# A decoder step on one core: attention taken by pairs of heads over all four query blocks, in a written order on the array, with its memory laid out by hand

## The chip, the core and the metric

The kernel runs on one core of one Trainium2 chip. The core has five engines that run their own instruction streams and meet by semaphores: PE (the matmul array; its weight loads are shown as PEld), DVE (vector), ACT (scalar activation), POOL (general) and SP (which issues transfers). The metric is the device time of one execution in microseconds (us). The three timed executions of the kernel before took 2037.08, 2037.58 and 2037.85 us; the median is 2037.58.

## The reference

One inference step of a decoder layer, for 512 prompt tokens with 16 learned tokens ahead of them, and for 8 sample tokens with a cache of 128 positions each. With D = 2048:

```
z = LN(x) @ w_in + b_in                      # columns: q 16 x 64 | k 4 x 64 | v 4 x 64 | u 1024
q, k = rope(q), rope(k)                      # the first 16 of 64 dims are rotated
s = q k^T / 8, masked to 128 positions back and self; m = max(max s, sink); p = exp(s - m)
attn = p v / (sum p + exp(sink - m))         # 4 heads share one k and v
d_g = mean over the last 2, 4, 8, 16 positions of u_g, minus u_g       # 4 groups of 256 channels
pool_g = (d_g @ w_pool_g) * scale
h1 = LN(alpha h + [attn, pool] @ w_o)
y  = LN(alpha h1 + (silu(h1 @ w_gate) * (h1 @ w_up)) @ w_down)         # inner width 5632
```

Outputs are y for prompt and sample rows, the last keys and values, and the last 15 rows of u. All is float32.

## The kernel before, in words

**Products.** Channels lie on the 128 partitions, tokens on the free axis. The 536 token columns (8 sample, 16 learned, 512 prompt) go as two halves of 276 and 260, and behind attention, without the learned ones, as two of 260. A float32 product is made of three products of the faster type fp32r: each weight and each operand is split into a leading and a trailing part, and `products` issues leading × leading (L97), weight leading × operand trailing (L98) and weight trailing × operand leading (L100). Weights are split while the kernel runs: 512 columns at a time, ACT casts the leading part (`wh`, L91) and DVE subtracts to get the trailing one (`wl`, L92). Both come from rings of WB = 7 tiles.

**Attention's stage.** After the first layer norm, its transposes and the blocks of keys and values come eight blocks of queries (`mm_q`; a block is 128 columns of w_in, that is a pair of heads) and eight of pool input (`mm_u`); each is 96 matmuls. DVE adds the bias to a block of queries (L345) and rotates it (L280 to L283). `attention` (L354) takes one pair of heads, in two half groups of two query blocks each: scores (L369, float32, 64 rows of the array for each of the two heads), maxima with the mask on DVE (L372), exponentials on ACT (L381), scaling (L392), transposes (`tp`, L398 to L406), a copy by ACT, values (`o`, L412). Half groups share two banks of PSUM for scores, one for transposes and one for values; four banks belong to the blocks. `pool_group` (L469) takes the windowed differences (`dh`, `dl`) of two blocks of u through the group's map (`pm`). `sample_attention` does the eight sample rows with very small matmuls.

**Behind it.** `out_proj` (L593) makes `o` for the two halves of the rows; `ln1` (L620) is a layer norm over partitions by matmuls with ones (mean L624, var L633, whose squares `sq` come from ACT), then DVE and POOL make the operands T1 to T4 of a Winograd form (L641 to L660, parts split at L618). Gate and up take two 128-column blocks and both halves of rows at once by seven products of 24 matmuls (class `Set`; p1 to p7). The second layer norm, that of half 1, stands beside NFILL = 8 parts `fill()`: products 1 and 2 of the first eight sets, which need only half 0. Then come 44 sets, the down projection in four chunks, and the closing layer norm.

**Order.** The Tile framework orders each engine's instructions by dependencies, priorities and a timeline of its own. On an engine they run in that order. In the stage of attention it is this that places scores, transposes and values inside the blocks of products.

Of the kernel before, what the change touches and what calls it, by code (L numbers as in the profile page):

```python
# [7 lines left out]
F32 = mybir.dt.float32  # L8
# [29 lines left out]
NFILL = 8  # L38
LP = 600
STEP = 6  # L40
WB = 7
NRAW = 5
NT = 6
NG = 56

# [4 lines left out]
HALF = [slice(0, HN), slice(HN, NTOK)]  # L50
DHALF = [slice(0, NS + 256), slice(NS + 256, NTOK)]
# [3 lines left out]
def hybrid_step(ctx, tc, xin, w_in, w_o, w_g, w_u, w_d, w_pool, par_d, cst_d, ident_d, ln2gb, kct_d, vc_d, hist_d,  # L55
# [3 lines left out]
    cp = ctx.enter_context(tc.tile_pool(name="cp", bufs=1))  # L59
    wp = ctx.enter_context(tc.tile_pool(name="wp", bufs=2))  # L60
    ap_ = ctx.enter_context(tc.tile_pool(name="ap", bufs=16))
    dp = ctx.enter_context(tc.tile_pool(name="dp", bufs=1, space=bass.MemoryType.DRAM))

# [10 lines left out]
    def row_tile(name, w=NTOK):  # L74
        """[128, 520] float32 from the shared ring."""
        return ap_.tile([P, NTOK], F32, tag="row", name=name, bufs=16)[:, :w]

    # ---------------------------------------------------------------- weights
# [6 lines left out]
    def split(s, name, lo=None):  # L85
        """float32 [128, <=512] -> its leading and trailing float32r parts."""
        n = s.shape[-1]
        wh = wp.tile([P, 512], F32R, tag="wh", name=f"wh_{name}", bufs=WB)[:, :n]
        wl = wp.tile([P, 512], F32R, tag="wl", name=f"wl_{name}", bufs=WB)[:, :n]
        with tc.high_priority(prio[0]):  # L90
            nc.scalar.copy(wh, s)  # L91
            (lo or nc.vector).tensor_sub(wl, s, wh.bitcast(F32))  # L92
        return wh, wl
# [29 lines left out]
    def rstd_of(pool, var, n, name):  # L123
        """1/sqrt(var + eps) with one Newton step."""
        w = var.shape[-1]
        if w < HN:
            ve, r, t = [pool.tile([P, 3], F32, tag=f"rs{i}", name=f"rs{i}_{name}", bufs=3)[:n, :w] for i in range(3)]
        else:
            ve, r, t = [pool.tile([P, HN], F32, tag="t", name=f"rs{i}_{name}", bufs=NT) for i in range(3)]
# [17 lines left out]
    # ================================================================ phase A  # L147
    mixf = {}
    with ExitStack() as sa:
        act = sa.enter_context(tc.tile_pool(name="act", bufs=1))  # L150
        pa = sa.enter_context(tc.tile_pool(name="pa", bufs=1))
# [14 lines left out]
        xe = [wp.tile([P, 1024], F32, tag="raw", name=f"xe{c}", bufs=NRAW) for c in range(2)]  # L166
# [29 lines left out]
        def stats_e():  # L196
            """The same on the scalar engine for the 20 + 4 rows: the mean, then the mean square about it."""
# [33 lines left out]
        def x_half(h):  # L231
# [5 lines left out]
            for k2 in range(KT // 2):  # L237
# [13 lines left out]
                for kk in range(2):  # L251
                    k = 2 * k2 + kk
                    c, ks = k // 4, slice((k % 4) * P, (k % 4 + 1) * P)
                    tp = aux_tile([P, 512], ["sc", "sc", "pt", "o"][k % 4], f"xt{h}_{k}", 2 if k % 4 < 2 else 1)
# [30 lines left out]
        # ---- keys and values  # L285
# [3 lines left out]
        ko = pa.tile([P, 256], F32, tag="pts", name="ko", bufs=2)  # L289
        kvs = pa.tile([P, 2, 256], F32, tag="pts", name="kvs", bufs=2)[:NS]  # L290
# [15 lines left out]
        nc.sync.dma_start(cst, cst_d)  # L306
        prio[0] = WPRIO
# [29 lines left out]
        # the sample rows' queries: the two heads of a block in columns of their own, zero in the other's rows  # L337
# [16 lines left out]
        def attention(t, q):  # L354
            kt = t // 4
            mixf[t] = row_tile(f"mixf{t}")
            for bh in range(2):
                nm_ = f"{t}_{bh}"
                s = pa.tile([P, 2, 2, 256], F32, tag="s", name=f"s{nm_}", bufs=2)
                st = pa.tile([P, 4, 2, 2], F32, tag="sst", name=f"sst{nm_}", bufs=2)  # L360
                mx, nm, den, es = st[:, 0], st[:, 1], st[:, 2], st[:, 3]
                sc = [aux_tile([P, 2, 256], "sc", f"sc{nm_}_{j}", 2) for j in range(2)]
                for bb in range(2):
                    b = 2 * bh + bb
                    n, k0 = (NB0, 0) if b == 0 else (256, C_P + P * (b - 1))
                    mask = cst[:, CM0:CM0 + NB0] if b == 0 else cst[:, CM1:CM1 + 256]
                    for j in range(2):
                        r = slice(64 * j, 64 * j + 64)
                        nc.tensor.matmul(sc[j][:, bb, :n], q[r, C_P + P * b:C_P + P * (b + 1)], kT[r, kt, k0:k0 + n],  # L369
                                         start=True, stop=True)  # L370
                    for j in range(2):
                        nc.vector.tensor_tensor_reduce(out=s[:, bb, j, :n], in0=sc[j][:, bb, :n], in1=mask, scale=1.0,  # L372
                                                       scalar=NEG, op0=ALU.add, op1=ALU.max,
                                                       accum_out=mx[:, j, bb:bb + 1])
                sink = [par[:, PSINK + HEAD_A[t] + 4 * j:PSINK + HEAD_A[t] + 4 * j + 1] for j in range(2)]
# [11 lines left out]
                o = aux_tile([P, 2, P], "o", f"o{nm_}", 1)  # L387
                for bb in range(2):
                    b = 2 * bh + bb
                    n = NB0 if b == 0 else 256  # L390
# [3 lines left out]
                    tp = aux_tile([P, 2, 2, P], "pt", f"tp{t}_{b}", 1)  # L394
                    pt = pa.tile([P, 2, 2, P], F32, tag="pts", name=f"pts{t}_{b}", bufs=2)
                    if b == 0:
                        for j in range(2):
                            nc.tensor.transpose(tp[:META, 0, j, :], s[:, 0, j, 0:META], ident)  # L398
                            nc.tensor.transpose(tp[:, 1, j, :], s[:, 0, j, C_P:C_P + P], ident)
                        nc.scalar.copy(pt[:META, 0], tp[:META, 0])  # L400
                        nc.scalar.copy(pt[:, 1], tp[:, 1])
                        chunks = [(4, META), (0, P)]
                    else:
                        for j in range(2):
                            for c in range(2):
                                nc.tensor.transpose(tp[:, c, j, :], s[:, bb, j, c * P:(c + 1) * P], ident)  # L406
                        nc.scalar.copy(pt, tp)
                        chunks = [(b - 1, P), (b, P)]
                    for j in range(2):
                        kv = 2 * kt + j  # L410
                        for c, (vch, kn) in enumerate(chunks):
                            nc.tensor.matmul(o[64 * j:64 * j + 64, bb, :], vtm[:kn, vch, kv * 64:kv * 64 + 64],  # L412
                                             pt[:kn, c, j, :], start=(c == 0), stop=(c == 1))
                nc.vector.tensor_copy(mixf[t][:, NS + 256 * bh:NS + 256 * (bh + 1)], o.rearrange("p a b -> p (a b)"))

        # ---- pooling; its rows in the order sample, meta, prompt
# [555 lines left out]
```

## Time and profile before

| | |
|---|---|
| median of three executions | 2037.58 us (2037.08 to 2037.85) |
| profiled execution: span | 2037.3 us |
| PE busy | 1980.5 us, 97% |
| DVE busy | 1394.9 us, 68% |
| ACT busy | 890.6 us, 44% |
| POOL busy | 71.5 us, 4% |
| first PE instruction | 19.9 us |
| first query block to the last pooling map | 95 to 391 us |
| output projection | 391 to 587 us |
| second layer norm, until PE runs at full rate | 587 to 674 us |

The only execution profiled has the span above; the timed ones include what lies around it. A row of the timeline gives start and duration of one instruction, engine, line, operation, output and inputs, and in brackets the idle time before it with what ended it. Durations of matmuls overlap, so the distance of starts is what one costs. A float32 matmul leaves two records, one of fp32r one. "granted clock" (PEclk) is the share of full speed that the array was given.

### The profile page before, as it was taken

How to read it: one execution, taken by the hardware profiler on the slowest of the kernel's cores; microseconds unless marked ns; L12 is line 12 of the kernel's file. 1: busy time of each engine (PE TensorE's matmuls, PEld its weight loads, DVE VectorE, ACT ScalarE, POOL GpSimd, SP SyncE). 2: the span in 40 equal slices, each digit the busy share in tenths (PEclk: the TensorE clock that was granted, in tenths of full speed). 3: DMA queues.
4: the chain of work that ended last, by engine and by line, in shares of the span. 5: the costliest groups of instructions: out<-in, count | busy, mean ns of one | idle time of the engine just before them, and what ended most of it. 6: DMA issues, size and time to landing. Idle time of an engine off the chain costs nothing.

```text
span 2037.3 us, 39750 instructions
## 1 busy us (share of the span) xinstructions
PE 1980.5 (97%) x16059; PEld 1928.7 (95%) x16059; DVE 1394.9 (68%) x2815; ACT 890.6 (44%) x1854; POOL 71.5 (4%) x71
## 2 busy tenths in 40 slices
PE   5999999999998999999999999999999999999996
PEld 4988888999998999999999999999999999999996
DVE  6655556765869998888788888888875342332586
ACT  6533344543646545445444545444543232222342
POOL 3100000000007100000000000000000000000000
PEclk9999999999999999999999999999999999999998
DMA  7722112375744454343333334333456343432554
GB/s 279 223 66 64 60 61 68 130 223 174 237 149 156 141 182 156 108 132 112 117 118 122 120 110 128 112 127 107 133 185 210 105 138 101 153 96 94 161 165 143
DMA packets 104968, 278.38 MB, mean 137 GB/s; under 512 B 12792, under 2 KB 35904, under 8 KB 104744
## 3 DMA queue, kind: packets, MB, share of 16 engines
q1 hardware_dynamic: 104784, 275.85, 41.6%
q8 instruction: 125, 2.05, 0.4%
q14 instruction: 59, 0.48, 0.1%
HBM read 250.93 MB, written 27.41 MB: 137 GB/s over the span
## 4 chain that ended last, share of the span: by engine, by line
PE 94%; DVE 4%; ACT 1%; issue 1%; DMA 1%; SPq 0%; DVEq 0%; ACTq 0%
PE p_u L100 7%; PE p_u L97 7%; PE p_u L98 7%; PE p_g L100 7%; PE p_g L98 7%; PE p_g L97 7%; PE d L100 6%; PE d L98 6%; PE d L97 6%; PE o L100 3%; PE o L97 3%; PE o L98 3%; PE mm_q L97 2%; PE mm_q L98 2%; PE mm_u L97 2%; PE mm_q L100 2%
## 5 line engine op out<-in xcount | busy, mean ns | idle before, releaser
L98 PE MATMUL d<-al,wh_d 128*128 128x260 f32 x1056 | 274.6, 282 | 0.0
L97 PE MATMUL d<-ah,wh_d 128*128 128x260 f32 x1056 | 273.8, 282 | 0.0
L92 DVE TENSOR_TENSOR wl_u<-raw_u,wh_u 128x512 fp32r<-128x512 f32 x316 | 212.1, 693 | 54.5 <-ACT wh_u L91 51.3
L91 ACT CAST wh_u<-raw_u 128x512 fp32r<-128x512 f32 x316 | 185.4, 620 | 113.9 <-DVE raw_u L692 106.4
L91 ACT CAST wh_g<-raw_g 128x512 fp32r<-128x512 f32 x284 | 164.6, 621 | 134.5 <-DVE raw_g L692 123.7
L92 DVE TENSOR_TENSOR wl_g<-raw_g,wh_g 128x512 fp32r<-128x512 f32 x284 | 192.0, 696 | 33.7 <-ACT wh_g L91 30.5
L100 PE MATMUL d<-ah,wl_d 128*128 128x260 f32 x1056 | 212.5, 283 | 0.0
L98 PEld LDWEIGHTS d<-al,wh_d 128*128 128x128 f32 x1056 | 198.3, 188 | 0.0
L97 PEld LDWEIGHTS d<-ah,wh_d 128*128 128x128 f32 x1056 | 198.0, 188 | 0.0
L100 PEld LDWEIGHTS d<-ah,wl_d 128*128 128x128 f32 x1056 | 162.5, 188 | 0.0
L91 ACT CAST wh_d<-raw_d 128x512 fp32r<-128x512 f32 x144 | 82.3, 583 | 174.5 <-PE d L100 140.0
L97 PE MATMUL o<-mh,wh_o 128*128 128x260 f32 x512 | 145.1, 286 | 0.0
L98 PE MATMUL o<-ml,wh_o 128*128 128x260 f32 x512 | 144.9, 284 | 0.0
L100 PE MATMUL o<-mh,wl_o 128*128 128x260 f32 x512 | 144.9, 284 | 0.0
L834 DVE TENSOR_TENSOR acc<-acc,d 128x260 f32<-128x260 f32 x64 | 24.3, 422 | 153.9 <-PE d L100 153.9
L692 DVE TENSOR_TENSOR raw_g<-raw_g,raw_g 128x512 f32<-128x512 f32 x152 | 103.4, 693 | 0.6
L692 DVE TENSOR_TENSOR raw_u<-raw_u,raw_u 128x512 f32<-128x512 f32 x152 | 102.4, 685 | 1.8 <-DMA raw_u<-in_w_u_dram 1.2
L98 PEld LDWEIGHTS o<-ml,wh_o 128*128 128x128 f32 x512 | 97.1, 190 | 0.1
L100 PEld LDWEIGHTS o<-mh,wl_o 128*128 128x128 f32 x512 | 97.1, 190 | 0.0
L97 PEld LDWEIGHTS o<-mh,wh_o 128*128 128x128 f32 x512 | 96.6, 190 | 0.1
L91 ACT CAST wh_o<-raw_o 128x512 fp32r<-128x512 f32 x128 | 73.3, 616 | 48.0 <-DMA raw_o<-in_w_o_dram 34.7
L92 DVE TENSOR_TENSOR wl_d<-raw_d,wh_d 128x512 fp32r<-128x512 f32 x144 | 86.9, 641 | 4.9 <-ACT wh_d L91 3.8
(496 smaller groups left out, 6464.9 us busy)
## 6 DMA issues: line engine op xcount, KB each, us to landing
raw_g<-in_w_g_dram SPq DMA_DIRECT2D x96, 512.0 KB, 4.5
raw_u<-in_w_u_dram SPq DMA_DIRECT2D x96, 512.0 KB, 4.1
raw_o<-in_w_o_dram SPq DMA_DIRECT2D x64, 512.0 KB, 4.6
raw_d<-in_w_d_dram SPq DMA_DIRECT2D x48, 512.0 KB, 3.6
a_d<-c_g SPq DMA_DIRECT2D x44, 260.0 KB, 2.1
af<-a_d SPq DMA_DIRECT2D x44, 260.0 KB, 4.0
raw_d<-in_w_d_dram SPq DMA_DIRECT2D x48, 192.0 KB, 2.4
raw_kv<-in_w_in_dram SPq DMA_DIRECT2D x16, 512.0 KB, 4.7
```

What stands on the lines that cost most here:

```text
L91: nc.scalar.copy(wh, s)
L92: (lo or nc.vector).tensor_sub(wl, s, wh.bitcast(F32))
L97: nc.tensor.matmul(o, wh, hi[j], start=first, stop=False)
L98: nc.tensor.matmul(o, wh, lo[j], start=False, stop=False)
L100: nc.tensor.matmul(o, wl, hi[j], start=False, stop=last)
L692: op(t[:, gs], a[:, gs], b[:, gs])
L834: nc.vector.tensor_add(t, t, o)
```

## The change

**Attention over all four query blocks.** `attention` becomes four functions. `att_scores` issues the eight score matmuls of a pair (four blocks, two heads) into four banks, `att_softmax` does the two half groups, `att_turn` the sixteen transposes and `att_values` the sixteen value matmuls into one bank. The blocks of products now have two banks instead of four, the transposes share the four of the scores.

**A written order.** `step(engine)` makes every instruction issued inside it depend, on that engine, on the last twelve of the step before, without a semaphore. The stage's PE work is written as such steps: first block of queries, scores of pair 0, then in each round a block, transposes of the pair, a block, and values of that pair with scores of the next. Pooling maps stand behind the transposes of rounds 3 and 5 and in round 7, and the sample rows' pieces in between.

**Memory by hand.** Instead of pools there are three regions cut into rings by offsets. The rings of `wh` and `wl` have 4 tiles in attention's stage and 5 behind it (7 before); the ring of `hb`, `sq` and the helpers of 1/sqrt 3 (6 before); NFILL is 6 (8 before), with three pairs of sets instead of four made ahead; transposed probabilities have 4 tiles (2), the differences `dh` and `dl` 3 (2). The rows of the input beyond four tiles of 128 no longer lie in the weight ring. The down projection's inputs go through the ring of the fills. What the kernel computes is the same.

```diff
-NFILL = 8
+NFILL = 6
-WB = 7
+WA = 4
+WB = 5
-NT = 6
+NT = 3
...
+    @contextmanager
+    def step(*engines):
+        block = nc.cur_bb.bb
+        last = block.instructions[-1]
+        yield
+        code = block.instructions
+        start = next(k for k in reversed(range(len(code))) if code[k] is last) + 1
+        new = {}
+        for i in code[start:]:
+            if i.engine in [e.engine for e in engines]:
+                new.setdefault(i.engine, []).append(i)
+                for j in behind.get(i.engine, ()):
+                    tc.add_manual_dep(i, j, mybir.DependencyInfo(mybir.DependencyClass.NoSync,
+                                                                 mybir.DependencyReason.DATA), reason="step")
+        behind.update({e: [i.name for i in v][-12:] for e, v in new.items()})
...
         def mm_tile(name):
-            return ps.tile([P, 512], F32, tag="mm", name=name, bufs=4)
+            return ps.tile([P, 512], F32, tag="mm", name=name, bufs=2)
...
+        def att_scores(t, q):
+            kt = t // 4
+            sc = [[aux_tile([P, 2, 256], "sc", f"sc{t}_{bh}_{j}", 4) for j in range(2)] for bh in range(2)]
+            for b in range(4):
+                n, k0 = (NB0, 0) if b == 0 else (256, C_P + P * (b - 1))
+                for j in range(2):
+                    r = slice(64 * j, 64 * j + 64)
+                    nc.tensor.matmul(sc[b // 2][j][:, b % 2, :n], q[r, C_P + P * b:C_P + P * (b + 1)],
+                                     kT[r, kt, k0:k0 + n], start=True, stop=True)
+            return sc
...
+        def att_turn(t):
+            pts[t] = []
+            for b in range(4):
+                s, bb = soft[t][b // 2], b % 2
+                tp = aux_tile([P, 2, 2, P], "sc", f"tp{t}_{b}", 4)
+                pt = pa.tile([P, 2, 2, P], F32, tag="pts", name=f"pts{t}_{b}", bufs=4)
...
-        qq = [q_block(0), q_block(1)]
-        for t in range(8):
-            attention(t, qq[t])
-            if t < 6:
-                qq.append(q_block(t + 2))
-            if t > 0:
-                pool_step(t - 1)
-        sample_attention()
-        pool_step(7)
+        block("q0")
+        order = ["q1 q2", "q3 u0", "q4 u1", "q5 u2", "q6 u3", "q7 u4", "u5 u6", "u7"]
+        for t in range(8):
+            with step(pe):
+                if t:
+                    att_values(t - 1)
+                sc = att_scores(t, qs.pop(t))
+                if t >= 6:
+                    next(sample)
+            att_softmax(t, sc)
+            done, us = us, []
+            if t == 7:
+                with step(pe):
+                    for u in done:
+                        next(u)
+                    next(pool_group(2))
+            for n, name in enumerate(order[t].split()):
+                if n == 1:
+                    with step(pe):
+                        att_turn(t)
+                        for u in done:
+                            next(u)
+                        if t == 6:
+                            next(sample)
+                    if t in (3, 5):
+                        with step(pe):
+                            next(pool_group((t - 3) // 2))
+                block(name)
...
-        zs = pb.tile([P, HN], F32, tag="t", name=f"zs{h}", bufs=NT)
+        zs = pb.tile([P, HN], F32, tag="zs", bufs=2)
```

Line numbers in the changed kernel: products L185, L186 and L188; trailing split L180; bias L433; rotation L367 to L370; scores L452; transposes L496 to L503; mean L770, var L779. Its buffers carry the names of the regions (`fr`, `rr`, `mid_a`, `mid_b`).

Three places of the engines' orders show what moves. First PE before, inside the fifth block of queries: `sc2` are scores of pair 2, `mm_q4` the block.

```order
L100 MATMUL mm_q4_1_2031<-xhi1_121,wl_q4_01_2063 128x260
L369 MATMUL sc2_1_0_1982<-kT_124,q2_1544 128x256
L97 MATMUL mm_q4_0_2030<-xhi0_120,wh_q4_01_2062 128x276
...
L98 MATMUL mm_q4_0_2030<-xlo0_122,wh_q4_10_2092 128x276
L369 MATMUL sc2_1_1_1983<-kT_124,q2_1544 128x256
L97 MATMUL mm_q4_1_2031<-xhi1_121,wh_q4_10_2092 128x260
```

And PE of the change, around the scores of pair 0, between the first and the second block of queries:

```order
L188 MATMUL mm_q0_0_902<-rr_61 128x276
L188 MATMUL mm_q0_1_903<-rr_61 128x260
L452 MATMUL sc0_0_0_1018<-mid_a_62 128x152 [waits DVE_49,Activation_49]
L452 MATMUL sc0_0_1_1019<-mid_a_62 128x152
L452 MATMUL sc0_0_0_1018<-mid_a_62 128x256
L452 MATMUL sc0_0_1_1019<-mid_a_62 128x256
L452 MATMUL sc0_1_0_1020<-mid_a_62 128x256
L452 MATMUL sc0_1_1_1021<-mid_a_62 128x256
L185 MATMUL mm_q1_0_1066<-rr_61 128x276
L186 MATMUL mm_q1_0_1066<-rr_61 128x276
```

Scores that stood alone among products now follow one another, and those of pair 0 stand ahead of the second block. Second, DVE of the change at that place, from the bias of the first block to its rotated queries:

```order
L433 TENSOR_SCALAR mid_a_62<-mm_q0_0_902,fr_60 128x276 [waits PE_49]
L433 TENSOR_SCALAR mid_a_62<-mm_q0_1_903,fr_60 128x260 [waits PE_49]
L180 TENSOR_TENSOR rr_61<-fr_60,rr_61 128x512 [waits Activation_49]
L367 STREAM_SHUFFLE fr_60<-mid_a_62 128x536 [waits DMAHW0_49,DVE_49]
L368 TENSOR_TENSOR fr_60<-fr_60,mid_a_62 128x536 [waits DVE_49]
L369 TENSOR_TENSOR mid_a_62<-mid_a_62 128x536
L370 TENSOR_TENSOR mid_a_62<-mid_a_62,fr_60 128x536 [waits DVE_49]
```

One split of weights stands among them, where there were two. Third, PE in the second layer norm: before,

```order
L100 MATMUL p1_g0_7126<-b11h2_4475,wl_g0_11_7146 128x260
L633 MATMUL var1_7044<-sq1_1_7050,onesd_67 128x260 [waits Activation_49]
L633 MATMUL var1_7044<-sq1_2_7054,onesd_67 128x260 [waits Activation_49]
L633 MATMUL var1_7044<-sq1_3_7058,onesd_67 128x260 [waits Activation_49]
L633 MATMUL var1_7044<-sq1_4_7062,onesd_67 128x260 [waits Activation_49]
L633 MATMUL var1_7044<-sq1_5_7066,onesd_67 128x260 [waits Activation_49]
L97 MATMUL p1_g0_7126<-b11h3_4477,wh_g0_11_7145 128x260
```

and in the change:

```order
L185 MATMUL p2_g0_6110<-mid_b_3823,rr_61 128x260
L779 MATMUL var1_6017<-fr_60 128x260 [waits Activation_49]
L186 MATMUL p2_g0_6110<-mid_b_3823,rr_61 128x260
L779 MATMUL var1_6017<-fr_60 128x260 [waits Activation_49]
L188 MATMUL p2_g0_6110<-mid_b_3823,rr_61 128x260
L185 MATMUL p2_g0_6110<-mid_b_3823,rr_61 128x260
L779 MATMUL var1_6017<-fr_60 128x260 [waits Activation_49]
```

The sum of squares now comes in pieces of mostly one matmul among the products of the fills.

More of the change, by code (lines that the diff above doesn't have):

```diff
@@ L409, in attention @@
-                    for j in range(2):
[L410 to L414, printed above, removed]
+                soft[t].append(s)
@@ new lines, in hybrid_step @@
+        with step(pe):
+            att_turn(7)
+            next(sample)
+        g3 = pool_group(3, True)
+        for p in range(2):
+            with step(pe):
+                next(g3)
+                next(us[0])
+                if p == 0:
+                    att_values(7)
+                    next(sample)
+    for p in (sp[0], act, pa):
+        p.close()
+    sp[:] = [Pool(rr), WB]
+    for t in ("wh", "wl"):
+        sp[0].ring(t, 512, F32R, WB)
+    pb, gp = Pool(fr), Pool(rr, Region("mid_b", F32R, MDW))
```

224 lines of the change are left out of this document (142 added, 82 removed).

## The prediction

> **What bounds the kernel now.** I read the page from the top, then the windows, the waits of PE, and single rows of the timeline. First the page: the busy shares, the slices of PE and of its granted clock, and the chain that ended last.
>
> ```profile
> span 2037.3 us, 39750 instructions
> PE 1980.5 (97%) x16059; PEld 1928.7 (95%) x16059; DVE 1394.9 (68%) x2815; ACT 890.6 (44%) x1854; POOL 71.5 (4%) x71
> PE   5999999999998999999999999999999999999996
> PEclk9999999999999999999999999999999999999998
> PE 94%; DVE 4%; ACT 1%; issue 1%; DMA 1%; SPq 0%; DVEq 0%; ACTq 0%
> ```
>
> PE is the bound, and 97% leaves only 57 us of idle. But "busy" hides two things: what PE does between its products, and at which clock. So next the windows, cut at the stages (95 first query block, 391 output projection, 587 second layer norm, 674 full rate again). Columns: PE, weight load, DVE, ACT and POOL busy with counts, then the granted clock.
>
> ```profile
> core 0: us, PE busy (x) PEld busy (x) DVE busy (x) ACT busy (x) POOL busy (x), PEclk, DMA share, GB/s
> 95.00:391.00 296.00, 294.01 (x2272) 257.51 (x2271) 166.53 (x530) 110.02 (x323) 0.00 (x0) 0.99 0.23 73
> ...
> 602.00:648.00 46.00, 43.19 (x344) 42.51 (x343) 45.06 (x71) 30.23 (x68) 26.30 (x26) 0.96 0.48 153
> 648.00:674.00 26.00, 18.29 (x98) 16.49 (x98) 26.00 (x29) 13.01 (x32) 22.90 (x23) 0.74 0.16 49
> 700.00:725.00 25.00, 25.00 (x211) 25.00 (x210) 24.20 (x48) 11.35 (x21) 0.00 (x0) 1.00 0.59 187
> ```
>
> The last row is the steady state: 211 products in 25 us, 0.1185 us each. Two stages are off it. In 95 to 391 PE is busy throughout with 257 us of weight loads in 294; that is the stage of attention. In 602 to 674 it lost time openly: 2.8 + 7.7 us idle, and 344 and 98 products that need 40.8 and 11.6 us at the steady rate were busy for 43.2 and 18.3, so 9.1 us went to a low clock. PE's waits from 391 to 700 name what ended them (total, times, longest):
>
> ```profile
> PE p_g L100 <- DVE wl_g L92: 4.0, 3, 3.4
> PE p_g L98 <- DVE t3l L618: 3.7, 3, 2.3
> PE var L633 <- ACT sq L632: 3.2, 2, 1.9
> PE p_u L100 <- DVE wl_u L92: 2.6, 1, 2.6
> PE mean L624 <- DVE zs L608: 1.0, 1, 1.0
> ```
>
> Waits for var and mean make up 4.2 us, of which 1.9 belong to the first layer norm (the longest); so 2.3 us more were lost just behind 587, and the second layer norm costs 21.9 us now.
>
> **The attention stage: what is removed.** PE's timeline, one head pair's score inside a query block, then scores of both heads together:
>
> ```profile
> 123.28 0.29 PE L97 MATMUL mm_q<-xhi,wh_q 128*128 128x276 f32 x1
> 123.50 0.70 PE L369 MATMUL sc<-kT,q 64*128 64x256 f32 x2
> 124.12 0.39 PE L98 MATMUL mm_q<-xlo,wh_q 128*128 128x276 f32 x1
> 124.35 0.28 PE L97 MATMUL mm_q<-xhi,wh_q 128*128 128x260 f32 x1
> ...
> 151.91 0.70 PE L369 MATMUL sc<-kT,q 64*128 64x256 f32 x4
> 152.54 0.39 PE L98 MATMUL mm_q<-xlo,wh_q 128*128 128x260 f32 x1
> ```
>
> Each float32 matmul leaves two records. Between 123.28 and 124.35 lie 1.07 us; the two products take 0.25, so the lone score cost 0.82. A pair on the two halves of the rows (x4) takes 0.63 from its start to the next product, no more than one alone. So 0.63 is the work, and about 0.19 the way out of the products and back. From the orders of both kernels I counted the runs of float32 work that stand inside the products, from the first query block to the last pooling map: 93 before, 20 now. 73 × 0.17 to 0.20 = 12.4 to 14.6 us; I take 12.4, as runs of transposes and values have no row that prices their switch. Scores that run one after the other: 38 of 256 columns become 24, which is 14 × 0.63 = 8.8 (the ten of 152 columns become eight, which I leave at nothing). The products, transposes and values are the same in number.
>
> The stage's own waits go too, since a pooling map now stands at least a block behind the differences it reads:
>
> ```profile
> PE pm L97 <- ACT dh L453: 1.6, 2, 1.0
> ...
> 289.40 0.74 PE L97 MATMUL pm<-dh,wh_pool 128*128 128x260 f32 x4 [0.96 <-ACT dh L453]
> ...
> 290.70:293.90 3.20, 3.20 (x16) 2.67 (x15) 2.69 (x13) 3.07 (x11) 0.00 (x0) 0.52 0.00 0
> ```
>
> That is 1.6 us of idle, and behind the second one 3.2 us at half clock, worth 1.3 (16 products instead of 27): 2.9 us.
>
> **What it adds there.** (a) The first query block is followed at once by its own scores, where before the second block covered the rotation. The row of DVE after the first block:
>
> ```profile
> 107.89 0.90 DVE L345 TENSOR_SCALAR zq<-mm_q,par 128x276 f32<-128x276 f32 x2 [4.29 <-PE mm_q L100]
> ...
> 111.37 0.68 DVE L92 TENSOR_TENSOR wl_q<-raw_q,wh_q 128x512 fp32r<-128x512 f32 x1
> 111.98 0.71 DVE L283 TENSOR_TENSOR q<-zq,zs_q 128x536 f32<-128x536 f32 x1
> ```
>
> From 107.89 to 112.69 (111.98 and 0.71) is 4.8 us with two splits of weights in it, 0.6 each; the new order has one there, so PE waits about 4.2 us, with every later product queued behind the score. What such a wait does to the clock is seen at the first layer norm:
>
> ```profile
> 491.63 0.71 PE L633 MATMUL var<-sq,onesd 128*128 128x260 f32 x2 [1.87 <-ACT sq L632]
> 491.98 0.56 PE L97 MATMUL o<-mh,wh_o 128*128 128x260 f32 x1
> ...
> 495.58 0.31 PE L98 MATMUL o<-ml,wh_o 128*128 128x260 f32 x1
> ```
>
> For 3.6 us products come every 0.22 us, a loss of 1.7 (16 or 17 products where 30 would go). So (a) is 6 us, bounds 4 and 8. (b) The maps have two banks of PSUM instead of four, so the second half of each waits for an evacuation by ACT; at 0.47 us each I put 0.8 on three of the four, 2.4 us (0 to 6). (c) Transposes must not come before the softmax is done. They stand one block of 96 products (some 11.9 us) and the eight scores (2.4) behind its start. Its work by rows:
>
> ```profile
> L372 DVE CUSTOM_DVE_ANT_0 s<-sc,cst 128x256 f32<-128x256 f32 x48 | 19.9, 422 | 22.0 <-PE sc L369 22.0
> L392 DVE TENSOR_SCALAR s<-s,sst 128x256 f32<-128x256 f32 x48 | 14.0, 349 | 0.1
> L381 ACT ACTIVATE s<-s,sst 128x256 f32<-128x256 f32 x48 | 23.9, 500 | 20.0 <-DVE sst L377 20.0
> L381 ACT ACTIVATION_READ_ACCUMULATOR s<-s,sst 128x1 f32 x64 | 12.1, 189 | 0.0
> ```
>
> Eight exponentials with their reads are 5.5 us on ACT, half of the maxima before them 2.0, the last scalings after them 1.4; with the splits, the rotation and the pooling sums that the order puts between on DVE I get 11 to 12.6 us of 14.3. No wait, but little room: 2.5 us for all eight rounds, bounds 0 and 9. Sum of the stage: −12.4 − 8.8 − 2.9 + 6 + 2.4 + 2.5 = −13.2, bounds about −21 and −4.
>
> The rule on gaps: the Trainium skill, TensorE: Matmul & The Clock Gate, section "HAM oscillation — how this bites in real kernels", asks only that no idle be longer than about 3.4 us. The rows disagree: 1.87 us and 0.96 us were enough for half clock. By the rule (a) alone would slow the clock and (b) would cost its idle only; by the rows (b) could cost 1.3 us more at each place, so that the sum of the stage would be −13.2 by the rule and at worst −9.3 by the rows.
>
> **The second layer norm.** Six parts of gate and up stand ready to fill it instead of eight, each two products of 24 matmuls: 96 × 0.1185 = 11.4 us of cover less. The squares come through a ring of three tiles instead of six, and the order spreads the sixteen matmuls of var over 97 products where 43 stood between: 54 × 0.1185 + 8 more switches × 0.19 = 7.9 us until 1/sqrt(var) can begin. PE works in that time, but behind var wait DVE's scaling of the rows, POOL's differences and the operands T2 to T4, on which all that follows the fills depends. Of PE's waits above, those for split weights and for T3's lower part all end on DVE. Its splits while POOL is silent (700 to 760) and busy (636 to 674):
>
> ```profile
> L92 DVE TENSOR_TENSOR wl_g<-s_g,wh_g 128x512 fp32r<-128x512 f32 x13 | 8.8, 687 | 1.2 <-ACT wh_g L91 1.2
> ...
> L92 DVE TENSOR_TENSOR wl_g<-s_g,wh_g 128x512 fp32r<-128x512 f32 x6 | 7.2, 1226 | 0.0
> ```
>
> DVE is full (45.1 of 46 us and 26.0 of 26), and its splits take 1.2 us instead of 0.69 while POOL runs. Two fills less take eight splits out of its row, 5.5 to 9.8 us. So the operands come between 2 us earlier and 8 later; I take no change, because the later start and the shorter row are of one size. Then the 11.4 us of cover are simply missing: +11.4, bounds +2 and +18. The lower one needs DVE's row to be the whole chain (then the operands come 9.8 earlier).
>
> **The rest.** The rings of split weights have four tiles in attention and five behind it instead of seven; a product of 24 matmuls (2.8 us) uses two, so five hold some 7 us of work, and DVE has 0.8 us of air in 25 (the row 700 to 725): nothing, bounds 0 and +5. The splits of the mixed rows wait for the last pooled block, whose input they overwrite; nine us of PE work stand between: +1 (0 to 3). The start loses its hold of the weight ring by 24 rows of the input: −1 to +1, nothing. Gate and up, down and the closing norm keep their work. In all −13.2 + 11.4 + 1 = −0.8: 2037.3 − 0.8 = 2036.5, and the median lies 0.3 above the profiled span. I say **2036**.
>
> **Rivals.** First, **the layer norm costs next to nothing**: DVE full speaks for it, the later var against. −13.2 + 2 + 1 gives 2027, and 2019 with the lower bound of attention.
>
> Second, on the other side, **the long runs of float32 work lower the clock**. Values of one pair, 1.2 to 2 us, and scores of the next, 2.4 us, now stand in one run, longer than any before, and scores use half of the rows. For it speaks the start, where PE transposes without a gap:
>
> ```profile
> 19.92 0.69 PE L256 MATMUL xt<-ident,x 128*128 128x128 f32 x2 [19.92 <-ACT x L222]
> ...
> 26.65 0.69 PE L256 MATMUL xt<-ident,x 128*128 128x128 f32 x2
> ...
> 47.56 0.44 PE L256 MATMUL xt<-ident,x 128*128 128x128 f32 x2
> ```
>
> After 6.7 us of transposing, a pair still takes 0.69 us, where later it takes 0.44. Against it: 0.63 us for scores in the middle of products, with full rate behind. If each of eight such runs is followed by 3.6 us at half clock, that is 8 × 1.7 = 13.6 us, which eats the whole gain: 2050. It decides from five rounds on. In the Trainium skill, the same page, "Part 4: PE-mode transpose", it is said that transposing doesn't count as busy for the clock; the rows of the start agree, and none shows it for scores.
>
> Third, **the softmax is late in every round** by about 1 us: +8, 2044; the 20.0 us that ACT waits for the maxima speak for it.
>
> **How the numbers follow.** The forecast's case, both large terms near their sums, has 0.45 and 2028 to 2045; the first rival 0.25, the second 0.22, the third 0.08. The kernel's three runs differ by 0.77 us, but 0.2% (4 us) is what I count as told apart. Faster: 0.17 + 0.24; same: 0.21 + 0.01 + 0.01 + 0.05; slower: 0.07 + 0.21 + 0.03. So 0.41, 0.28 and 0.31. The range takes half of the first rival and most of the second: 2020 to 2051.
>
> **What would show it.** Right: output projection beginning some 13 us earlier than 391, one idle of 4 us before the first scores, transposes without a wait, and the stretch from the second mean to the full rate some 86 us long with about 33 us lost. Wrong: a clock of 0.5 behind runs of values and scores, "tp <- DVE s" high among PE's waits, T3 ready 9 us sooner, or waits for split weights in the steady state.

## The result, and the profile after

The changed kernel takes 2055.93 us (median of four, 2053.07 to 2064.51) where the kernel before took 2037.71 beside it: 1.0092 times as long, 95% interval 1.0079 to 1.0106. It is slower, and it lies outside the range that was given. The page of the changed kernel, with the lines that answer to those of before:

```profile
span 2053.9 us, 40465 instructions
PE 1967.0 (96%) x16059; PEld 1934.2 (94%) x16059; DVE 1426.7 (69%) x2805; ACT 936.5 (46%) x1856; POOL 69.3 (3%) x71
PE   5999999999986899999999999999999999999996
PEclk9999999999997999999999999999999999999998
PE 87%; DVE 6%; DMA 3%; ACT 1%; issue 1%; POOL 1%; SPq 0%; DVEq 0%; POOLq 0%; ACTq 0%
```

PE is busy 13.5 us less than before, and the span is 16.6 us longer: 30 us went into idle. The slices of PE put it in one place, the twelfth to fourteenth (565 to 719 us at 51.35 us each); in the middle one the granted clock falls too. The chain now has 3% of transfers, which it had not.

The windows of the changed kernel, cut at the same points of its work (attention's stage, output projection, second layer norm and its parts, and what was the steady state before). The first starts at 95 us as before, though the first query block now begins at 97.53 us instead of 94.59:

```profile
95.00:369.00 274.00, 268.42 (x2284) 256.19 (x2282) 173.90 (x545) 119.85 (x343) 0.00 (x0) 0.98 0.25 79
369.00:566.00 197.00, 194.13 (x1583) 191.85 (x1582) 134.21 (x258) 102.92 (x194) 0.00 (x0) 1.00 0.63 205
566.00:582.00 16.00, 13.72 (x80) 12.57 (x81) 10.05 (x24) 8.26 (x19) 0.00 (x0) 0.89 0.34 114
582.00:660.00 78.00, 55.80 (x362) 53.15 (x360) 66.42 (x96) 42.06 (x96) 47.99 (x48) 0.83 0.35 109
660.00:745.00 85.00, 73.87 (x547) 71.37 (x547) 65.19 (x118) 34.48 (x64) 0.18 (x1) 0.91 0.42 139
```

The output projection begins at 369 us where it began at 391: a gain of 22, more than forecast. As the first query block began 2.9 us later, the stage itself is some 25 us shorter. The output projection is as it was (197). Then PE idles 2.3, 22.2 and 11.1 us in the last three rows, and the last of them lies behind all work of the layer norm: POOL is done, and still PE waits. What it waits for, from the second mean on for 190 us (total, times, longest):

```profile
PE p_g L188 <- DVE rr L180: 12.2, 5, 5.1
PE p_u L185 <- ACT rr L179: 8.8, 4, 3.7
PE p_g L185 <- ACT rr L179: 6.1, 5, 2.7
PE p_g L185 <- ACT rr L763: 3.8, 1, 3.8
PE p_u L188 <- DVE rr L180: 2.5, 2, 2.3
```

Before, waits for the casts of weights (L91, now L179) stood at 0.2 us in this part; they are 14.9 now.

A measure for what follows: 190 us from the second mean, less the matmul records in it times the steady 0.1185 us. Not every record is such a product (a float32 matmul leaves two), so only differences count; the two traces hold equally many, 16059. Here the two kernels:

```profile
587.76:777.76 190.00, 177.45 (x1372) 173.42 (x1373) 176.87 (x305) 102.23 (x216) 49.20 (x48) 0.96 0.48 155
```

```profile
566.90:756.90 190.00, 155.28 (x1084) 148.99 (x1085) 149.29 (x251) 88.41 (x185) 48.17 (x48) 0.88 0.39 125
```

190 − 1372 × 0.1185 = 27.4 before, and 61.5 now: **34.1 us more are lost behind the mean**. −22 and +34 leave +12; a further 1.5 us are lost where the down projection begins and 3 at its end, which makes the 16.6.

### The profile page after: what moved, and what is told of

Same layout as the page of the kernel before. It is cut to its first block, busy times and chain, and to the rows that moved or that the text cites. A ratio compares the mean times of both kernels' runs of the same rounds, so it can differ in the third digit from the quotient of the medians.

```text
span 2053.9 us, 40465 instructions
## 1 busy us (share of the span) xinstructions
PE 1967.0 (96%) x16059; PEld 1934.2 (94%) x16059; DVE 1426.7 (69%) x2805; ACT 936.5 (46%) x1856; POOL 69.3 (3%) x71
## 4 chain that ended last, share of the span: by engine, by line
PE 87%; DVE 6%; DMA 3%; ACT 1%; issue 1%; POOL 1%; SPq 0%; DVEq 0%; POOLq 0%; ACTq 0%
PE p_u L185 7%; PE p_u L188 7%; PE p_u L186 6%; PE p_g L185 6%; PE p_g L186 6%; PE p_g L188 6%; PE d L186 6%; PE d L188 6%; PE d L185 6%; PE o L185 3%; PE o L188 3%; PE o L186 3%; DVE rr L180 2%; PE mm_q L185 2%; PE mm_u L188 2%; PE mm_u L185 2%
## 5 line engine op out<-in xcount | busy, mean ns | idle before, releaser
L179 ACT CAST rr<-fr 128x512 fp32r<-128x512 f32 (+1 forms) x1084 | 660.9, 612 | 964.4 <-PE d L186 263.9
L180 DVE TENSOR_TENSOR rr<-fr,rr 128x512 fp32r<-128x512 f32 (+1 forms) x1068 | 722.0, 684 | 446.0 <-ACT rr L179 438.9
L838 DVE TENSOR_TENSOR fr<-fr 128x512 f32<-128x512 f32 x352 | 239.1, 695 | 25.1 <-DMA fr<-in_w_u_dram 14.8
L185 PE MATMUL p_g<-rr 128*128 128x260 f32 x836 | 239.6, 287 | 9.7 <-ACT rr L179 5.9
L188 PE MATMUL p_g<-rr 128*128 128x260 f32 x836 | 237.5, 285 | 8.7 <-DVE rr L180 8.6
L185 PE MATMUL p_u<-rr 128*128 128x260 f32 x836 | 238.1, 285 | 2.3 <-ACT rr L179 2.3
L188 PE MATMUL p_u<-rr 128*128 128x260 f32 x836 | 235.9, 283 | 3.0 <-DVE rr L180 3.0
L186 PE MATMUL p_g<-rr 128*128 128x260 f32 x792 | 225.5, 285 | 0.0
L186 PE MATMUL p_u<-rr 128*128 128x260 f32 x792 | 224.2, 283 | 0.0
L185 PEld LDWEIGHTS p_g<-rr 128*128 128x128 f32 x836 | 159.4, 191 | 10.9 <-ACT rr L179 6.8
L188 PEld LDWEIGHTS p_g<-rr 128*128 128x128 f32 x836 | 159.8, 192 | 9.6 <-DVE rr L180 9.5
L188 PEld LDWEIGHTS p_u<-rr 128*128 128x128 f32 x836 | 158.5, 190 | 3.5 <-DVE rr L180 3.4
L185 PEld LDWEIGHTS p_u<-rr 128*128 128x128 f32 x836 | 157.9, 189 | 3.0 <-ACT rr L179 3.0
L186 PE MATMUL d<-rr 128*128 128x260 f32 x608 | 158.7, 283 | 0.0
L185 PE MATMUL d<-rr 128*128 128x260 f32 x608 | 158.1, 281 | 0.0
L186 PEld LDWEIGHTS p_g<-rr 128*128 128x128 f32 x792 | 151.1, 191 | 0.3
L186 PEld LDWEIGHTS p_u<-rr 128*128 128x128 f32 x792 | 149.9, 189 | 0.1
L185 PE MATMUL o<-rr 128*128 128x260 f32 x512 | 145.9, 285 | 0.0
L188 PE MATMUL o<-rr 128*128 128x260 f32 x512 | 144.9, 284 | 1.0 <-DVE rr L180 1.0
L186 PE MATMUL o<-rr 128*128 128x260 f32 x512 | 144.4, 282 | 0.0
L186 PE MATMUL p_u<-mid_b,rr 128*128 128x260 f32 x440 | 126.6, 288 | 0.0
L186 PE MATMUL p_g<-mid_b,rr 128*128 128x260 f32 x440 | 126.5, 288 | 0.0
```

The source lines that it names most:

```text
L185: nc.tensor.matmul(o, wh, hi[j], start=first, stop=False)
L186: nc.tensor.matmul(o, wh, lo[j], start=False, stop=False)
L188: nc.tensor.matmul(o, wl, hi[j], start=False, stop=last)
L838: op(t[:, gs], a[:, gs], b[:, gs])
```

## Experiments

All times are medians; the kernel before, run beside each, stood at 2037.7 to 2039.3. Loss means the measure above, as a difference to the kernel before (changed kernel: +34.1).

**Early loads.** In the changed kernel the down projection's inputs are loaded into the ring of the fills, which is free once the first sets are done. SP's queue there, and then what DVE and PE wait for:

```profile
680.03 0.33 SPq L916 DMA_DIRECT2D a_d<-fr  x1
682.07 0.33 SPq L952 DMA_DIRECT2D fr<-a_d  x1
682.78 0.94 SPq L171 DMA_DIRECT2D fr<-in_w_u_dram  x2
683.99 0.33 SPq L916 DMA_DIRECT2D a_d<-fr  x1
687.00 0.33 SPq L171 DMA_DIRECT2D fr<-in_w_u_dram  x1
690.88 0.33 SPq L952 DMA_DIRECT2D fr<-a_d  x1
691.30 0.38 SPq L171 DMA_DIRECT2D fr<-in_w_u_dram  x1
```

```profile
695.17 1.29 DVE L838 TENSOR_TENSOR fr<-fr 128x512 f32<-128x512 f32 x2 [4.79 <-DMA fr<-in_w_u_dram]
```

```profile
696.64 0.38 PE L185 MATMUL p_u<-mid_b,rr 128*128 128x260 f32 x1 [3.03 <-ACT rr L179]
```

A load of `a_d` (L952) waits until the write ahead of it (L916) has landed, the next load of weights (L171) is issued only at 691.30 behind it, DVE waits 4.8 us for that and PE 3.0. Before, the first of these loads was issued at 1485 us. The edit:

```diff
-        up_out(o[1], go, i)
+        if i == NPAIR - 3:
+            with step(nc.sync):
+                up_out(o[1], go, i)
+        else:
+            up_out(o[1], go, i)
...
-    a_cur = load_a(0)
+    with step(nc.sync):
+        a_cur = load_a(0)
```

> The changed kernel, with one thing moved: the loads of the down projection's first inputs (and all behind them) are ordered on SP's queue behind the write of the third pair of blocks from the end, instead of following the first writes at 682 to 760 us. Theory 1 (each of the first six such loads stands in SP's queue until the write it reads has landed, and the loads of weights queue behind it; this costs the 14 us lost between 98 and 175 us behind the second layer norm's mean): 10 to 14 us less than the changed kernel, some 2043 us, no wait of that line on SP before 1450 us, and the loss behind the mean stops growing at about 38 us. Theory 2 (the weight rings of five tiles starve PE there, with or without those loads): no more than 3 us less.

2055.41 us, ratio 1.0076 (1.0059 to 1.0093); loss +29.4. In the trace 4.7 us of the loss are gone, in the medians 0.5: four runs went from 2050.28 to 2057.39, and the changed kernel's from 2053.07 to 2064.51, so a few us can't be told here. The trace is that of the fastest of the four, 5 us under their median, so its 4.7 is rather too much. Theory 1 fell: the early loads are a small part, not 10 to 14 us. The time is what theory 2 forecast, but that doesn't show its cause, the five tiles of split weights.

**The wait before the first scores.** On top of that the second query block ahead of the first scores:

```diff
         block("q0")
-        order = ["q1 q2", "q3 u0", "q4 u1", "q5 u2", "q6 u3", "q7 u4", "u5 u6", "u7"]
+        block("q1")
+        order = ["q2 q3", "q4 u0", "q5 u1", "q6 u2", "q7 u3", "u4 u5", "u6", "u7"]
...
```

> As af_late, and the second block of queries stands ahead of the scores of pair 0, as it did before the change (all later rounds move up by one block; round 6 keeps one block, so values of pair 6 follow its transposes at once). If the wait of 4.4 us for the rotated queries and the slow clock behind it cost what their rows say (4.4 and 1.5 to 1.7), 5 to 6 us less than af_late, less about 1 us for the copies in round 6. If something else holds PE there, no change.

2052.55 us, 1.0065 (1.0047 to 1.0083). (In this kernel the transposes of two pooled blocks read a tile that the next block had filled already, so some of the pooled history's rows are others; the work is the same.) The wait for the rotated queries is gone, but PE stands elsewhere: 2.6 us for the sample rows behind a copy of the pooled history, and 1.7 at the output projection for a cast. The difference to af_late is within their spreads.

**The sizes of the rings, in the kernel before.**

```diff
-NFILL = 8
+NFILL = 6
```

> The kernel before, with six parts of gate and up to fill the second layer norm instead of eight, and nothing else. If missing cover is the price (96 products of 0.1185 us), +11 us, some 2049 us, with the loss behind the second mean 32 us instead of 21. If DVE's shorter row brings the operands sooner, +2 to +5.

```diff
-WB = 7
+WB = 5
```

> The kernel before, with five tiles in each ring of split weights instead of seven. By my forecast nothing in the steady state; at most 5 us. If the shorter ring is what starves PE behind the layer norm and in the last chunk of the down projection, +8 us and more, with waits of products for split weights and casts between 600 and 760 us and behind 1960.

Both edits and `NT = 3` instead of 6 in one kernel:

> The kernel before with all three shorter rings (six fills, five tiles of split weights, three of squares), and nothing else. If the prices add (7.2 to 8.5 for the fills, 8.7 for the weights, and something for the squares), +17 to +22 us, 2055 to 2061: then the rings account for half or more of what the changed kernel loses behind attention (34 us). If one hides the other, +9 to +11.

Fills: 2046.26 us, 1.0035 (1.0021 to 1.0048), +7.2, loss +7.8. Weights: 2047.83 us, 1.0043 (1.0026 to 1.0060), +8.7, loss +4.5, and 3 us at the end of the down projection. All three: 2055.03 us, 1.0077 (1.0060 to 1.0094), +15.8, loss +9.1; 7 us more go at the end. The first and the third lie between the two values expected; the second is as its rival case had it. So the missing cover costs less than its 11.4 us of products, and the prices behind the mean don't add. And the ring of weights isn't free: at the end of the down projection PE waits for it, after the change too (b_wb5 waits there for splits as well, 1.7 us in all). In the changed kernel:

```profile
PE d_7h L188 <- DVE rr L180: 0.8, 1, 0.8
```

The sizes explain 9 of 34 us, if they cost behind the new attention what they cost behind the old one.

**Attention alone.** The kernel before with its pools, the new attention and its order put in, and WB = 5 throughout:

> The kernel before with its pools and rings, into which only the new attention is put: pairs of heads over all four query blocks, the written order, the banks of PSUM, four tiles of transposed probabilities and three of the differences. The rings of split weights have five tiles throughout (with six the memory does not suffice); fills are eight, the ring of squares six tiles. Theory (attention is worth −22 us as the trace of the changed kernel has it, five tiles +8.7 as measured by b_wb5, and all else of the loss belongs to the memory laid by hand): 2037.7 − 22 + 8.7 = 2024, between 2020 and 2029, faster than both. Rival (the loss is one of the attention stage's early end, since half of the second layer norm's work is then closer): 2045 and more.

**2018.35 us, ratio 0.9895 (0.9881 to 0.9910)**, faster than both, and below the range expected. Its second mean begins at 563.05 us, 24.7 earlier than in the kernel before (587.76) and 3.9 earlier than in the changed one (566.90): the changed memory costs a little ahead of the mean too. Its loss behind the mean is +2.4:

```profile
563.05:753.05 190.00, 175.43 (x1352) 170.95 (x1353) 172.69 (x303) 103.57 (x218) 54.59 (x48) 0.96 0.45 150
```

Attention's gain stands by itself, and that the stage ends early does not bring the loss. With six fills as well:

> As att_wb5, with six fills instead of eight (pools as before the change, five tiles of split weights, six of squares). If two fills less cost what they cost the kernel before (+7 us), 2025; then sizes alone explain about 8 of the 20 us that a_rawpool_af still loses between the second norm's mean and the steady state, and some 12 are of the other rings laid by hand. If 2032 and more, the sizes explain nearly all of it once attention ends early.

2024.49 us, 0.9930 (0.9913 to 0.9946); loss +8.2. Two fills cost 6 us here, 7 in the kernel before. So fills and five tiles of split weights are cleared of the rest. It lies in the memory laid by hand, or in the ring of squares, which has six tiles here and three in the changed kernel.

**The turn of the weight tiles.** A region laid by hand gives tile k mod 5 by the order of the program; a pool gives the tile that is free when the order is made. First the fixed turn alone, in the kernel before:

```diff
-        raw = wp.tile([P, 1024], F32, tag="raw", name=f"raw_{name}", bufs=NRAW)[:, :src.shape[-1]]
+        raw = raw_tile()[:, :src.shape[-1]]
...
```

`raw_tile` gives five tiles one after the other, also to the sums S1, S2, S4 and, at the start, to 24 rows of the input.

> The kernel before, with one thing changed: the five tiles that weights are loaded into are made once and used in turn by the order of the program (tile k mod 5), as the regions laid by hand do it, where the pool gives any tile that is free. All sizes stay. If the fixed turn is what the changed kernel pays beside its shorter rings (a load must wait for one certain tile, that of the sums S1, S2, S4, which lives longest, and all later loads and writes queue behind it on SP), the loss behind the second norm's mean rises from 20 to 30 and more us: +8 to +25 us, 2046 to 2062. If a fixed turn is harmless, within 2 us.

2073.53 us, 1.0165 (1.0150 to 1.0180): +35, more than expected. 12.1 us are lost by the second mean (599.86 us instead of 587.76), 7.5 of them ahead of the first query block (102.09 us instead of 94.59), and 18.0 in the 190 us behind it, 22.6 if 210 us are taken. (The 24 rows of the input that lie in two of these tiles are overwritten in this kernel, so its values are others.) Then the other way, the changed kernel with only these tiles from a pool:

```diff
-    wp.ring("raw", 1024, F32, NRAW)
+    wr = ctx.enter_context(tc.tile_pool(name="wr", bufs=NRAW))
...
```

> The changed kernel, with the tiles for loaded weights taken from a pool of five again (the region is smaller by as much); the rest by hand as it was. If the fixed turn of these tiles is what costs, 8 to 20 us less: 2036 to 2047, with the loss behind the mean near that of b_all (30 us) instead of 52. If it is another ring (rows, fills) or the sizes alone, within 3 us of 2055.

2044.99 us, 1.0031 (1.0020 to 1.0043): 11 us less than the changed kernel; loss +23.2. Both directions point the same way, though not to one size: 11 us here, 22.6 behind the mean there. This edit also takes the tiles out of a region that is one large tile; in b_rawfix they are five tiles of their own, and the turn alone does it. With the early loads moved too:

> As a_rawpool, and the loads of the down projection's first inputs late as in af_late. Theory (fixed turn, early loads and short rings are all that is lost): the changed kernel's attention with the loss of b_all, 2039 − 22 + 16 = 2033, 2028 to 2038. If the early loads cost nothing once weights come in time, as a_rawpool.

2043.06 us, 1.0017 (1.0008 to 1.0027); loss +17.9, 5.3 less in the trace; in the medians 2 us, about what its ten runs (2038.39 to 2046.28) can tell. The profiled run lies 3 us under its median here too. The time is above the 2028 to 2038 of the theory, so more is lost than the turn, the early loads and the sizes. The two traces, a_rawpool first:

```profile
566.39:756.39 190.00, 161.48 (x1176) 155.46 (x1177) 161.12 (x270) 95.12 (x198) 46.51 (x48) 0.91 0.42 139
...
567.60:757.60 190.00, 163.62 (x1221) 157.78 (x1222) 166.13 (x280) 98.16 (x203) 46.51 (x48) 0.93 0.40 132
```

The rows tiles from a pool as well, and then the second query block first:

> As a_rawpool_af, and the 16 rows tiles (inputs, mixed rows, sums of the layer norm, results of the sets) from a pool too. If their fixed turn holds the first sets back behind the layer norm (a set's results wait for the first rows of the norm, in order), 5 to 12 us less than a_rawpool_af: 2031 to 2038. If not, within 2 us of 2043.

> As a_rawrow, and the second block of queries ahead of the scores of pair 0. The wait of 4.4 us and the slow clock behind it go: 4 to 6 us less than a_rawrow, less 1 us for the copies in round 6, so −3 to −5. If PE is held by the next thing at the same place (the early rounds have one block less to cover the softmax), no change.

2041.51 us, 1.0011 (1.0002 to 1.0021), loss +16.7: the rows are not it. And 2041.48 us, 1.0013 (1.0004 to 1.0023): no change. With the second query block first, PE is 8 us ahead by the middle of the stage (2 of them from before it) and loses them in its last rounds, where it now waits:

```profile
PE tpu L561 <- DVE mid_a L479: 3.4, 1, 3.4
PE smpt L633 <- DVE fr L627: 1.6, 1, 1.6
PE smpt L634 <- DVE fr L629: 0.8, 1, 0.8
PE tpu L561 <- ACT fr L565: 0.5, 1, 0.5
```

Those rounds have one block of products less to cover their work; no run separates this from the rest. With the attention of att_wb5 the second query block first was not measured.

**What attention's gain consists of.** The scores of a pair in another order, four blocks of one head and then four of the other (base att_wb5):

```diff
-            for b in range(4):
-                n, k0 = (NB0, 0) if b == 0 else (256, C_P + P * (b - 1))
-                for j in range(2):
+            for j in range(2):
+                for b in range(4):
+                    n, k0 = (NB0, 0) if b == 0 else (256, C_P + P * (b - 1))
```

> As att_wb5, with the eight scores of a pair of heads in another order: four blocks of one head, then four of the other, so that no two neighbours use different halves of the rows. If two heads' scores run at once only as neighbours, each of eight rounds has 3 x 0.63 + 0.46 = 2.35 us more: +18.8 us over att_wb5. If the time of scores does not depend on it, no change.

2023.01 us, 0.9921 (0.9906 to 0.9935): +4.7, a quarter of what was expected. The eight scores of pair 1 in att_wb5, and in att_jouter:

```profile
174.01 1.82 PE L382 MATMUL sc<-kT,q 64*128 64x152 f32 x16
```

```profile
175.43 2.62 PE L382 MATMUL sc<-kT,q 64*128 64x152 f32 x16
```

Eight scores in a run take 1.82 us, and 2.62 where no two heads are neighbours: 0.80 more, 6.4 in eight rounds. At 0.63 each pair they would have taken 2.35, and 4.7 one by one. So neighbours on the two halves of the rows do gain, but less than was thought, as scores of one head in a run are also much shorter than 0.63.

And the changed kernel without the written order:

```diff
-                for j in behind.get(i.engine, ()):
+                for j in ():
```

> The changed kernel without the written order (the scheduler places the steps' instructions; grouping, banks and memory are the same). If the gain of attention is in the grouping, no change of its stage (within 5 us). If it is in the order, the stage ends 10 to 20 us later than in the changed kernel, as runs of float32 work are again cut up among the products.

2054.66 us, 1.0075 (1.0060 to 1.0090). The stage does not get longer, its output projection begins 2.4 us sooner (366.58 us instead of 368.94). The scheduler keeps the scores together without the written order, in runs of eight of 1.82 to 1.83 us, so this kernel doesn't test scattered scores with the new banks. The gain is in the grouping, as the rows of the scores below show; the written order adds nothing here.

## Why the prediction was wrong

**Attention, −13.2 forecast, −22 measured: the mechanism was right, the size off.** Scores of before and after by their groups, from the first query block to the output projection:

```profile
L369 PE MATMUL sc<-kT,q 64*128 64x256 f32 x96 | 27.0, 427 | 0.2 <-DVE sst L372 0.2
...
L369 PE MATMUL sc<-kT,q 64*128 64x152 f32 x32 | 5.6, 366 | 0.0
```

```profile
L452 PE MATMUL sc<-mid_a 64*128 64x256 f32 x96 | 13.0, 406 | 0.0
...
L452 PE MATMUL sc<-mid_a 64*128 64x152 f32 x32 | 4.4, 347 | 4.4 <-DVE mid_a L370 4.4
```

The scores alone went from 32.6 to 17.4 us: −15.2 where the term for pairs had −8.8. The step "0.63 is the work" failed: 0.63 us passed from a score that stood alone, or from a pair, to the next product; in a run one score takes 0.23 (1.82 for eight), and 0.33 without a neighbour of the other head (2.62 for eight). Transposes and values gave back some 8 us more in the same view (23.7 to 19.6 and 29.7 to 25.4 us), part of the 12.4 for switches. The costs, by their terms: (a) 6 us forecast, and the row below has 4.36 us of idle and scores that take 3.21 instead of 1.82; (b) 2.4 forecast, and PE waits 0.3 in all for maps; (c) 2.5 forecast, and no transpose waits. These are all waits of PE in 95 to 369 us:

```profile
PE sc L452 <- DVE mid_a L370: 4.4, 1, 4.4
PE mm_u L188 <- DVE rr L180: 0.9, 1, 0.9
PE pm L185 <- DVE mid_a L467: 0.3, 1, 0.3
...
114.86 3.21 PE L452 MATMUL sc<-mid_a 64*128 64x152 f32 x16 [4.36 <-DVE mid_a L370]
```

The start, taken at nothing (−1 to +1), took the other way 2.9 us: the first query block begins at 97.53 us instead of 94.59.

**The second rival came true at two places only.** Behind values and scores alone full rate follows: after the first row below, products start at 242.17, 242.40, 242.53 and 242.65. Where the sample rows' very small matmuls (L601 here, L646 at the end of the stage) stand in the same run, half clock follows, without an idle time of PE ahead of it:

```profile
240.41 1.82 PE L452 MATMUL sc<-mid_a 64*128 64x152 f32 x16
...
305.81 3.74 PE L601 MATMUL smT<-fr 128*128 128x8 f32 x32
...
310.00:312.00 2.00, 2.00 (x11) 2.00 (x11) 1.90 (x7) 2.00 (x8) 0.00 (x0) 0.50 0.68 205
...
362.91 4.06 PE L514 MATMUL o<-mid_a 16*64 16x128 f32 x32
```

The run up to 309.40 is 8.1 us of values, scores and small matmuls, and for 3.4 us behind it products come every 0.22 us. At the end of the stage the last values take 4.06 us where those of an earlier round took 2.66. That is some 3 us of the 13.6 that the rival had; with the slow scores of pair 0 it makes the stage's granted clock 0.98.

**The second layer norm, +11.4 forecast with bounds +2 and +18.** Its later start was sized right: 1/sqrt(var) begins 22.6 us behind the mean instead of 14.5, 8.1 for the 7.9 worked out. Up to 100 us behind the mean the loss is some 18 us more than before, at the upper bound. "Two fills less take splits out of DVE's row" was to pay for the later start. Cover missing by itself costs 6 to 8 us (b_nfill6, att_w5f6), not 11.4, so some 3 to 5 us were paid, by that or otherwise, and of the 18 all sizes together explain no more than the 9 of b_all.

**"The rest: nothing" is the step that decided it.** It held that five tiles of split weights hold 7 us of work and that gate and up "keep their work". Of 34 us lost behind the mean, some 11 belong to the fixed turn of the weight tiles (a_rawpool, and b_rawfix from the other side), 2 to 5 to the loads that stand in SP's queue 800 us early (by the medians and by the traces), 9 to shorter rings, 1 to 2 to the rows; **7 to 11 stay open**, among the rings still laid by hand (split weights, fills, squares), which were not tried one by one. "Waits for split weights in the steady state", named as a sign of being wrong, came: they are the waits for L179 and L180 above. Behind them stand weights that land late. DVE's waits for landings, in the 190 us from the second mean, before and after:

```profile
DVE raw_u L692 <- DMA raw_u<-in_w_u_dram: 1.2, 1, 1.2
DVE s_g L692 <- DMA raw_g<-in_w_g_dram: 0.8, 1, 0.8
...
DVE fr L838 <- DMA fr<-in_w_u_dram: 13.1, 3, 5.5
DVE fr L838 <- DMA fr<-in_w_g_dram: 7.5, 3, 3.0
```

That is 2.0 us before and 20.6 after; with the fixed turn in the kernel before (b_rawfix) it is 11.5, with all sizes short (b_all) 1.6. The prediction counted instructions on PE and DVE and the sizes of rings, and no row of SP's queue. The rows of the changed kernel in 660 to 745 us:

```profile
SPq L171 <- DVE rr L180: 25.4, 6, 11.0
SPq L171 <- DVE fr L838: 18.3, 9, 5.5
SPq L916 <- DVE fr L915: 16.5, 4, 8.3
SPq L171 <- DVE fr L899: 9.8, 1, 9.8
SPq L952 <- DMA a_d<-fr: 9.8, 4, 3.5
```

Loads of weights wait for splits (L180) and for the sums S1 to S4 (L838) to leave a tile, writes of the gated rows (L916) stand 16.5 us in the same queue, and loads of what was just written another 9.8; what is behind them comes late. With all memory from pools att_wb5 loses 2.4 us in its 190. The trace of before had such waits, though not as waits of PE. From SP's queue of before, 585 to 800 us:

```profile
SPq L82 <- DVE wl_u L92: 41.1, 11, 11.0
SPq L82 <- DVE wl_g L92: 33.2, 8, 14.2
...
SPq L82 <- DVE raw_g L692: 3.7, 2, 3.5
```

Loads of weights waited 74 us for DVE's splits to free a tile, and came in time; for the sums they waited 4.6 us in all (3.7 here and 0.9 for the other weights). In the same stretch of the changed kernel it is 55.8 for splits and 52.8 for sums. Those were the rows to price, with what stands behind them. A wait of the queue does no harm by itself: b_all has 19.0 us of waits for sums in 682 to 767 us, with PE at full rate (700 products in 85 us). That the order of the queue turns the fixed turn into late weights is read from these rows and from the place around 691 us shown above; the runs show only what the turn costs.

**The end.** 3 us at the end of the down projection go with the shorter ring of weights (b_wb5 loses the same there), inside the bound of 5 that was given, but taken at nothing.

## What to carry to other kernels

Here a float32 score alone among products of another kind cost 0.82 us, and in a run of eight 0.23; gather such work first. In the orders between the runs that were tried here the time then stayed the same within 3 us. When buffers are laid by hand, a ring's turn becomes part of the schedule: price it at the queue that fills the ring, and look which load or write stands ahead of which, and whether what is behind them still lands in time. A change that gains in one stage and pays in another is worth taking apart: its attention, put into the old memory, is 1.05% faster than before, while the whole is 0.92% slower.

## What was not expected of the hardware

Eight float32 scores of 64 rows that follow each other took 1.82 us, where one alone in a stream of products cost 0.82. After an idle time of 4.36 us the same eight took 3.21. Behind 8.1 us of float32 values, scores and matmuls of 8 columns, with no idle time among them, the granted clock was 0.50.
